# Third block of the seven-product FFN heads into the hand-written order, with earlier side sums and an earlier copy of x

## The chip, the cores and the metric

One Trainium2 chip, one of its cores. The metric is the device time of one execution of the whole program in microseconds (us). TensorE (PE in the profile) multiplies; VectorE (DVE), ScalarE (ACT) and GpSimd (POOL) work on what it needs and gives; the DMA queues of SyncE (SP) and of POOL move data. Each engine works through its own queue of instructions in order, and engines wait for one another by semaphores.

## The reference

A trunk of four layers on x, 512 positions by 1024 channels, float32. Each layer adds a mixer's output to x (layers 0 and 3: S5, layer 1: gated linear attention, layer 2: differential attention), and then a SwiGLU feed-forward (FFN) of hidden size 2816; a last rmsnorm ends it.

```python
def swiglu_ffn(h, w_gate_up, w_down):
    g, u = jnp.split(h @ w_gate_up, 2, axis=-1)
    return (jax.nn.silu(g) * u) @ w_down

for l in range(DEPTH):
    ...
    x = x + mixer(rmsnorm(x, ...))
    h = rmsnorm(x, ffn_norm_g[l])
    x = x + swiglu_ffn(h, ffn_w_gate_up[l], ffn_w_down[l])
```

The change concerns the FFNs of layers 1, 2 and 3: their first three of 11 blocks of 256 hidden channels.

## The kernel before

**Precision.** A float32 product is made of three products in the faster format fp32r: each operand is split into a high part (a copy with rounding, on ACT; for weights `high`, L334) and a low part (the operand minus its high part, on DVE; for weights `low`, L338), and high x high, high x low and low x high are summed. So every weight tile that TensorE uses costs one ACT and one DVE instruction of 128x1024 first, and the two matmul groups that need only the high part can start before the low part is there: each product's first two matmuls take the high part of the weights, the third the low part.

**Seven products.** Layer 0's FFN is `ffn_plain`. The FFNs of layers 1, 2 and 3 (`ffn`, L712) multiply 2x2 partitioned matrices with seven products instead of eight. `Sides` keeps the four quarters of the normed input, transposed (F), and makes the sums of them that the scheme needs (`total`, L191; high and low parts L212 and L217). `seven_block` (L571) holds the steps of one block: loads of weight quarters from DRAM (L599 by SP, or `staged`, L324), sums of quarters either by a DMA that accumulates (POOL's queue, L602) or on DVE (`add`, L659), splits, the products `one` to `seven` (each 24 matmuls of 128x256 on L566), and the evacuations: `one_out` (ACT copy, L638), `two_out` (DVE, L645), `gate1` and `gate2` (DVE multiply by the norm's scale L611, ACT SiLU L612), `five_out` and `six_out` (ACT copies, L656, L670), `seven_out` (DVE, L676), `three_out` (DVE subtraction L683 and multiply L684), and in `four_out` the multiply L693 and the split of the result into high and low (`act`, ACT copies L703 and DVE subtractions L704; in layer 2 in four pieces, since the columns change order there). PSUM banks: a for products one, six, seven, four; c for five and three; d for two.

**Order of the work.** In each of these FFNs the first two blocks, a and b, stand in an order written out by hand: `plan` in `ffn` is a list of step names, and all five queues (PE, ACT, DVE, SP, POOL) run in the order in which the steps issue instructions. `finish`, `square`, `diag`, `spread`, `rows`, `flush` and the `total`, `high`, `low` steps without a block letter belong to the norm and the sides. After `self.hand()` a planner orders the instructions of blocks 2 to 10 by due times. The blocks are done in groups of 4, 4 and 3; behind each group the down projection (`gemm_b`) runs. Weight tiles come from pools: `wst` (3 buffers, staged quarters), `whl` (5 buffers, split quarters), three `slots`, and rooms lent from `act` buffers, the quarters F once the sides are made, and the gain's buffer. A block's first quarter of weights can be loaded and split ahead of the FFN (`ahead`, L165), which also makes the first side sum, `total("3")`, when two blocks are done.

**x's copy.** Layer 2's FFN leaves its columns in another order for the S5 layer behind it. For that `turn_x` (L800) copies x to DRAM (L804, 2048 KB) and back with the rows in the other order (L806), and the norm's scale the same way (L808, L810), all four on POOL's queue; the way back waits for the way there. Before, this is issued behind the accumulating load of the third block's product three (`self.added`).

**Ahead of the head.** The attention's last product of layer 2 is ordered by hand as well: its four row tiles are evacuated by `evac` and the FFN's first weights made ready by `ahead(1)` between the products (`between`). Layers 1 and 3 call `ahead(2)` in the last product of their mixers (L1521, L1734).

Of the kernel before, what the change touches and what calls it, by code (L numbers as in the profile page):

```python
# [11 lines left out]
F32 = mybir.dt.float32  # L12
F32R = mybir.dt.float32r
# [132 lines left out]
class Sides(Left):  # L146
# [18 lines left out]
    def ahead(self, n):  # L165

        w = [self.tr.staged(self.quarter(0, 0, b), 4, 256) for b in range(len(self.heads), len(self.heads) + n)]
        self.heads += [self.tr.halves(y, 4, 256) for y in w]
        if len(self.heads) == 2:
            self.total("3")  # L170
# [92 lines left out]
class Trunk:  # L263
# [307 lines left out]
    def seven_block(self, fp, slots, left, wgu, b, turn):  # L571
# [20 lines left out]
        def load(name, q, half, plus=None, room=None):  # L592
# [8 lines left out]
            if plus:  # L601
                self.added = nc.gpsimd.dma_start(w[:], left.quarter(*plus, b), accum_op=ALU.add)  # L602
# [78 lines left out]

        def three_out():
            v.tensor_tensor(keep["r2"][:], bank["c"][:], keep["r2"][:], op=ALU.subtract)  # L683
            v.tensor_tensor(keep["r1"][:], keep["r1"][:], keep["r2"][:], op=ALU.mult)  # L684
# [4 lines left out]

        def four_out():  # L690
            g2 = T("g2")
            scaled(g2, bank["a"], 1)
            v.tensor_tensor(keep["r5"][:], g2[:], keep["r5"][:], op=ALU.mult)  # L693
            act = fp.tile([P, 2, 2, SEQ], F32R, tag="act", name="act", bufs=4)
            for th, k in enumerate(("r1", "r5")):
                src = keep[k][:].rearrange("p (j n) -> p j n", j=2)
                if turn:
                    dst = act[:].rearrange("p z j (b h m) -> p z j h m b", b=4, h=2)[:, :, :, th]
                    src = src.rearrange("p j (m b) -> p j m b", b=4)
                else:  # L700
                    dst = act[:].rearrange("p z j (h n) -> p z j h n", h=2)[:, :, :, th]
                for j in range(2) if turn else (slice(None),):
                    nc.scalar.copy(dst[:, 0, j], src[:, j])  # L703
                    v.tensor_tensor(dst[:, 1, j], src[:, j], dst[:, 0, j].bitcast(F32), op=ALU.subtract)  # L704
            return act
# [3 lines left out]
            add, six, six_out, seven, seven_out, three, three_out, four, four_out,  # L709
        )}  # L710

    def ffn(self, l, left, after=None, turn=False, aside=None):  # L712
# [5 lines left out]
        with self.tc.tile_pool(name=f"ffn{l}", bufs=1, reuse_waits="tile") as fp:  # L718
# [11 lines left out]
            f = blocks[:2]  # L730
            if l == 3:
                left.open(fp, ("4", "3", "22"))
            for w, n, *room in (
# [6 lines left out]
                split21a one:a split21b square flush one:b total1 one_out:a finish high1 low1 total2 split1a high2 low2  # L740
                one_out:b two:a two:b split1b high3 two_out:a five:a add22a highSa two_out:b lowSa five_out:a five:b
                add22b highSb diag lowSb low3 split3a six:a spread five_out:b rows six:b six_out:a split3b seven:a
                six_out:b total4 split22a high4 low4 seven:b seven_out:a split22b three:a seven_out:b gate1:a gate1:b
                high22 low22 three:b add21a highFa add21b lowFa highFb lowFb four:a four:b three_out:a three_out:b
            """
            for step in plan.split():
                name, _, n = step.partition(":")
                if n:
                    f["ab".index(n)][name]()
                elif name[-1] in "ab":  # L750
                    word = next(w for w in ("split", "add", "high", "low") if name.startswith(w))
                    w = name[len(word) : -1]
                    f["ab".index(name[-1])][word]({"S": "1", "F": "1"}.get(w, w))
# [4 lines left out]
                elif name == "flush":  # L758
                    self.flush()
                else:  # L760
# [4 lines left out]
            F = left.freed()  # L765
            slots[:] = [F[0], F[1], slots[0], F[2], left.g[:].rearrange("p (k n) -> p k n", n=256), F[3]] + slots[1:]
            b0 = 0
            for nb in (4, 4, 3):
                acts = []
                for n in range(b0, b0 + nb):  # L770
                    b = blocks[n]
                    if n > 1:
                        for w in ("direct", "room1", "room22", "room21", "summed"):
                            b[w]()
                    if turn and n == 2:

# [1013 lines left out]
    def diff(self, l, left, after):  # L1790
# [4 lines left out]
        with self.tc.tile_pool(name="diff", bufs=1) as p:  # L1795
# [268 lines left out]
            for t in range(2, NT):  # L2064
# [6 lines left out]
                if t == 2:  # L2071
                    nxt[0].ahead(1)
# [65 lines left out]
```

## Time and profile before

| what | us |
|---|---|
| median of 3 runs | 2381.13 (2380.29 to 2392.86) |
| the profiled execution | 2382.31 |
| span of its trace | 2380.6 |
| mean granted TensorE clock | 0.982 of full |
| PE busy | 2269.0 |
| DVE busy | 1487.1 |
| ACT busy | 1073.0 |
| POOL busy | 266.8 |

The span is what the hardware profiler saw from the first to the last instruction; the execution's time holds 1.7 us more around it. A row of a timeline reads: start, duration of the stretch, engine, line, operation, tile written <- tiles read, shapes, how many instructions; in brackets how long the engine had been idle before it and which instruction released it ("<-ACT whl L334" is the end of a high part of weights). A row of a group has count, busy time, mean ns of one, and idle time before with its releasers. A row of DMA issues has count, size and median us from issue to landing. In the trace the products are known by their bank and sides: "c<-side" is three, "d<-sides" two, "a<-sides" one or, with "side", six, seven or four, and "c<-side" in a block's second place five.

### The profile page before, as it was taken

The page shows a single profiled execution, that of the slowest core. Times are in us where ns is not written, and L with a number is a line of the kernel's source. Part 1 is how long each engine was busy: PE and PEld are TensorE (multiplying, and loading weights), DVE is VectorE, ACT ScalarE, POOL GpSimd, SP SyncE. Part 2 cuts the span into 40 slices and gives each one's busy share as a digit, 9 for nine tenths or more (in the row PEclk, how much of TensorE's full clock was granted, in tenths as well). Part 3 has the DMA queues.
Part 4 walks back from the last instruction along what each step waited for, and adds up shares of the span by engine and source line. Part 5 has one row for each costly group of instructions (what it writes and reads, how often), then busy time and mean ns, then how long its engine had stood idle before and what let it go on. Part 6 is the DMA issues. An engine that isn't in the chain of part 4 may idle for free. (4 is left out here: it accounts for less than half of the span.)

```text
span 2380.6 us, 35208 instructions
## 1 busy us (share of the span) xinstructions
PE 2269.0 (95%) x14055; PEld 1962.8 (82%) x14055; DVE 1487.1 (62%) x2311; ACT 1073.0 (45%) x1749; POOL 266.8 (11%) x335
## 2 busy tenths in 40 slices
PE   4799999999999999999999998989999899999997
PEld 3578888788877789898987887888989788999996
DVE  7774565555443459585753666875847874967674
ACT  4463445444352346252544665653635233634442
POOL 3330100111000011010001221110000000101000
PEclk9699999999999999999999999999999899999999
DMA  4123344544332258564345465694732645666521
GB/s 110 34 52 138 95 138 143 166 129 166 118 103 85 71 143 208 137 177 124 111 142 117 107 133 145 170 243 115 195 98 89 214 158 150 170 179 154 162 76 67
DMA packets 275502, 317.42 MB, mean 133 GB/s; under 512 B 45653, under 2 KB 214377, under 8 KB 274058
## 3 DMA queue, kind: packets, MB, share of 16 engines
q1 hardware_dynamic: 227210, 238.14, 31.9%
q0 software_dynamic: 48128, 77.02, 15.7%
q8 instruction: 111, 1.82, 0.3%
q14 instruction: 53, 0.43, 0.1%
HBM read 275.92 MB, written 23.99 MB: 126 GB/s over the span
## 5 line engine op out<-in xcount | busy, mean ns | idle before, releaser
L338 DVE TENSOR_TENSOR whl<-wst,whl 128x1024 fp32r<-128x1024 f32 x294 | 359.0, 1223 | 363.1 <-ACT whl L334 362.3
L334 ACT CAST whl<-wst 128x1024 fp32r<-128x1024 f32 x294 | 308.4, 1050 | 530.5 <-PE acc L353 354.8
L566 PE MATMUL a<-side,whl 128*128 128x256 f32 x2376 | 291.2, 279 | 14.2 <-ACT r L638 6.0
L566 PEld LDWEIGHTS a<-side,whl 128*128 128x128 f32 x2376 | 281.4, 190 | 16.2 <-ACT whl L334 6.9
L351 PE MATMUL acc<-whl,act 128*128 128x512 f32 x704 | 276.5, 393 | 0.7 <-DVE g L611 0.7
L353 PE MATMUL acc<-whl,act 128*128 128x512 f32 x704 | 276.9, 393 | 0.0
L352 PE MATMUL acc<-whl,act 128*128 128x512 f32 x704 | 275.6, 391 | 0.0
L566 PE MATMUL c<-side,whl 128*128 128x256 f32 x1584 | 192.4, 278 | 3.6 <-DVE whl L338 3.6
L566 PEld LDWEIGHTS c<-side,whl 128*128 128x128 f32 x1584 | 186.9, 189 | 4.0 <-DVE whl L338 4.0
L351 PEld LDWEIGHTS acc<-whl,act 128*128 128x128 f32 x704 | 132.2, 188 | 30.9 <-DVE g L611 1.9
L352 PEld LDWEIGHTS acc<-whl,act 128*128 128x128 f32 x704 | 132.2, 188 | 28.8
L353 PEld LDWEIGHTS acc<-whl,act 128*128 128x128 f32 x704 | 132.3, 188 | 27.9
L351 PE MATMUL any<-hT,whl 128*128 128x512 f32 x384 | 151.7, 395 | 0.0
L352 PE MATMUL any<-hT,whl 128*128 128x512 f32 x384 | 149.6, 390 | 0.0
L353 PE MATMUL any<-hT,whl 128*128 128x512 f32 x384 | 149.6, 389 | 0.0
L351 PE MATMUL acc<-whl,hT 128*128 128x512 f32 x352 | 143.8, 408 | 1.1 <-ACT whl L334 0.6
L352 PE MATMUL acc<-whl,hT 128*128 128x512 f32 x352 | 138.6, 394 | 1.0 <-DVE whl L338 1.0
L353 PE MATMUL acc<-whl,hT 128*128 128x512 f32 x352 | 139.0, 395 | 0.0
L338 DVE TENSOR_TENSOR whl<-halves,whl 128x1024 fp32r<-128x1024 f32 x72 | 87.7, 1222 | 32.5 <-ACT whl L334 32.5
L352 PE MATMUL acc<-whl,zT 128*128 128x512 f32 x256 | 103.9, 406 | 4.1 <-DVE whl L338 4.1
L334 ACT CAST whl<-halves 128x1024 fp32r<-128x1024 f32 x72 | 75.3, 1052 | 69.2 <-PE acc L353 26.7
L351 PE MATMUL acc<-whl,zT 128*128 128x512 f32 x256 | 102.8, 406 | 2.7 <-ACT zT L468 2.7
(438 smaller groups left out, 4185.1 us busy)
## 6 DMA issues: line engine op xcount, KB each, us to landing
wst<-in_ffn_w_gate_up_dram SPq DMA_DIRECT2D x110, 512.0 KB, 4.0
wst<-in_ffn_w_down_dram SPq DMA_DIRECT2D x88, 512.0 KB, 3.7
halves<-in_ffn_w_gate_up_dram SPq DMA_DIRECT2D x42, 512.0 KB, 5.9
slot<-in_ffn_w_gate_up_dram SPq DMA_DIRECT2D x39, 512.0 KB, 6.6
wst<-in_ffn_w_gate_up_dram POOLq DMA_DIRECT2D x33, 512.0 KB, 6.4
wst<-in_s_w_glu_dram SPq DMA_DIRECT2D x32, 512.0 KB, 3.6
spill<-opsp POOLq DMA_DIRECT2D x8, 2048.0 KB, 8.7
wst<-in_gla_w_in_dram SPq DMA_DIRECT2D x24, 512.0 KB, 3.6
```

Source lines behind the costliest of these rows:

```text
L334: self.nc.scalar.copy(hl[:, 0], w[:])
L338: self.nc.vector.tensor_tensor(hl[:, 1], w[:], hl[:, 0].bitcast(F32), op=ALU.subtract)
L351: mm(out, lh, rh, start=first, stop=False)
L352: mm(out, lh, rl, start=False, stop=False)
L353: mm(out, ll, rh, start=False, stop=last)
L566: mm(o, hl[:, x, k, c], side[:, y, k], start=first and not (j or k or n), stop=k == 3 and n == 2, skip_group_check=True,)
```

## The change

- The plan goes on through the third block, c: its loads, its splits, its products (in the order one, five, two, six, seven, three, four), its side sums and most of its evacuations are written out. Two of c's quarters are loaded into F(0,0) and F(0,1) (steps F0 and F1), which come free inside the plan.
- `three_out` and `four_out` are split into steps. The evacuations of a and b (gate1, three_sub, three_mul, gate2, half1, four_mul, half2) stand behind c's first weight splits, instead of ahead of four:a or right behind four:b.
- Side 22's high and low (high22, low22) and the sums for four (add21a, add21b) stand ahead of the gate1 steps.
- total3 is no longer part of `ahead`: in layers 1 and 3 it is called behind `ahead(2)`, in layer 2 it stands in the plan behind one:b.
- x's copy stands in the plan behind five:b.
- In the attention's last product the evacuations of the first two tiles stand two matmul groups sooner, and `ahead(1)` stands behind the evacuations of the third and fourth tile.

The number of instructions on each engine is the same in both kernels. In the order on TensorE only block c differs: before, the planner had placed it as one, five, two, six, with two and six interleaved, then seven, three, four; after the change four:c's first two matmuls are followed by the first two of block d's one.

```diff
--- before.py
+++ after.py
@@ -166,8 +166,6 @@
 
         w = [self.tr.staged(self.quarter(0, 0, b), 4, 256) for b in range(len(self.heads), len(self.heads) + n)]
         self.heads += [self.tr.halves(y, 4, 256) for y in w]
-        if len(self.heads) == 2:
-            self.total("3")
 
     def open(self, pool, names):
 
@@ -599,7 +597,7 @@
                 nc.sync.dma_start(W[name][:], left.quarter(q, half, b))
             w = W[name]
             if plus:
-                self.added = nc.gpsimd.dma_start(w[:], left.quarter(*plus, b), accum_op=ALU.add)
+                nc.gpsimd.dma_start(w[:], left.quarter(*plus, b), accum_op=ALU.add)
 
         def done(name):
             if name not in lent:
@@ -679,34 +677,60 @@
             product("4", "22", bank["c"], False)
             done("22")
 
+        def three_sub():
+            v.tensor_tensor(keep["r2"][:], bank["c"][:], keep["r2"][:], op=ALU.subtract)
+
+        def three_mul():
+            v.tensor_tensor(keep["r1"][:], keep["r1"][:], keep["r2"][:], op=ALU.mult)
+
         def three_out():
-            v.tensor_tensor(keep["r2"][:], bank["c"][:], keep["r2"][:], op=ALU.subtract)
-            v.tensor_tensor(keep["r1"][:], keep["r1"][:], keep["r2"][:], op=ALU.mult)
+            three_sub()
+            three_mul()
 
         def four():
             product("22", "1", bank["a"], False)
             done("1")
 
+        def gate2():
+            keep["g2"] = T("g2")
+            scaled(keep["g2"], bank["a"], 1)
+
+        def four_mul():
+            v.tensor_tensor(keep["r5"][:], keep["g2"][:], keep["r5"][:], op=ALU.mult)
+
+        def half(th, k):
...
+            for j in range(2) if turn else (slice(None),):
+                nc.scalar.copy(dst[:, 0, j], src[:, j])
+                v.tensor_tensor(dst[:, 1, j], src[:, j], dst[:, 0, j].bitcast(F32), op=ALU.subtract)
+
+        def half1():
+            half(0, "r1")
+
+        def half2():
+            half(1, "r5")
+            return keep["act"]
+
+        def act():
+            return keep["act"]
+
         def four_out():
...
+            gate2()
+            four_mul()
+            half1()
+            return half2()
 
...
@@ -727,7 +751,8 @@
                 lent = room()
             self.jobs = aside(fp) if aside else iter(())
             blocks = [self.seven_block(fp, slots, left, wgu, b, turn) for b in range(FFN_HIDDEN // 256)]
-            f = blocks[:2]
+            f = blocks[:3]
+            F = left.freed()
             if l == 3:
                 left.open(fp, ("4", "3", "22"))
             for w, n, *room in (
@@ -737,46 +762,50 @@
                 f[n][w](*room)
 
             plan = """
-                split21a one:a split21b square flush one:b total1 one_out:a finish high1 low1 total2 split1a high2 low2
-                one_out:b two:a two:b split1b high3 two_out:a five:a add22a highSa two_out:b lowSa five_out:a five:b
-                add22b highSb diag lowSb low3 split3a six:a spread five_out:b rows six:b six_out:a split3b seven:a
-                six_out:b total4 split22a high4 low4 seven:b seven_out:a split22b three:a seven_out:b gate1:a gate1:b
-                high22 low22 three:b add21a highFa add21b lowFa highFb lowFb four:a four:b three_out:a three_out:b
+                split21a one:a split21b square flush one:b total3 total1 one_out:a finish high1 low1 total2 F0 room1:c
+                split1a high2 low2 one_out:b two:a two:b split1b high3 two_out:a five:a add22a highSa two_out:b lowSa
+                five_out:a five:b turn add22b highSb diag lowSb low3 split3a six:a spread five_out:b rows six:b six_out:a
+                split3b seven:a direct:c six_out:b total4 F1 split22a high4 low4 seven:b seven_out:a split22b high22 low22
+                room22:c three:a room21:c high11c add21a highFa add21b lowFa highFb three:b lowFb summed:c seven_out:b
+                four:a low11c high1c gate1:a three_sub:a four:b three_sub:b low1c one:c
+                three_mul:a gate2:a half1:a four_mul:a half2:a split21c one_out:c five:c add22c gate1:b highSc three_mul:b
+                lowSc two:c five_out:c six:c split3c gate2:b half1:b four_mul:b half2:b two_out:c gate1:c
+                six_out:c seven:c split22c seven_out:c three:c add21c highFc three_sub:c lowFc three_mul:c four:c
             """
+            if l != 2:
+                plan = plan.replace("total3", "")
             for step in plan.split():
                 name, _, n = step.partition(":")
                 if n:
-                    f["ab".index(n)][name]()
-                elif name[-1] in "ab":
+                    f["abc".index(n)][name]()
+                elif name in ("F0", "F1"):
+                    slots.append(F[int(name[1])])
+                elif name[-1] in "abc":
                     word = next(w for w in ("split", "add", "high", "low") if name.startswith(w))
                     w = name[len(word) : -1]
-                    f["ab".index(name[-1])][word]({"S": "1", "F": "1"}.get(w, w))
+                    f["abc".index(name[-1])][word]({"S": "1", "F": "1"}.get(w, w))
                 elif name in ("finish", "diag", "spread", "rows"):
                     getattr(left, name)()
                 elif name == "square":
                     left.square(NT - 1, 1)
                 elif name == "flush":
                     self.flush()
+                elif name == "turn":
+                    r = self.turn_x(left.r) if turn else r
                 else:
                     word = next(w for w in ("total", "high", "low") if name.startswith(w))
                     getattr(left, word)(name[len(word) :])
             self.hand()
 
-            F = left.freed()
-            slots[:] = [F[0], F[1], slots[0], F[2], left.g[:].rearrange("p (k n) -> p k n", n=256), F[3]] + slots[1:]
+            slots[:] = [F[2], *slots[:2], left.g[:].rearrange("p (k n) -> p k n", n=256), F[3]] + slots[2:]
             b0 = 0
             for nb in (4, 4, 3):
                 acts = []
                 for n in range(b0, b0 + nb):
                     b = blocks[n]
-                    if n > 1:
+                    if n > 2:
                         for w in ("direct", "room1", "room22", "room21", "summed"):
                             b[w]()
-                    if turn and n == 2:
-
-                        with self.tc.issue_after(self.added.ins):
-                            r = self.turn_x(left.r)
-                    if n > 1:
                         for step in ("one", "one_out", "five", "five_out"):
                             b[step]()
                         b["add"]("22")
@@ -784,7 +813,7 @@
                             b[step]()
                         b["add"]("21")
                         b["four"]()
-                    acts.append(b["four_out"]())
+                    acts.append(b["four_out"]() if n > 1 else b["act"]())
                     next(self.jobs, None)
                 stat = lambda k, part, t: acts[k // 2][:, part, k % 2, t * P : (t + 1) * P]
                 if nb == 3 and after is not None:
@@ -1518,7 +1547,7 @@
                         evac_b(t, accs[t])
                 else:
                     self.gemm_b(stat, wg, KT, D + d * 512, evac_b)
-                ahead = (lambda: nxt.ahead(2)) if L and d else None
+                ahead = (lambda: (nxt.ahead(2), nxt.total("3"))) if L and d else None
                 self.gemm_b(stat, wg, KT, d * 512, evac_a, tail=4 if d else 0, ahead=ahead)
         return nxt
 
@@ -1731,7 +1760,7 @@
             for d in range(2):
                 self.gemm_b(
                     so, wo, KT, d * 512, self.add_x(d, nxt), tail=4 if d else 0, between=() if d else late,
-                    ahead=(lambda: nxt.ahead(2)) if d else None,
+                    ahead=(lambda: (nxt.ahead(2), nxt.total("3"))) if d else None,
                 )
         return nxt
 
@@ -2058,8 +2087,8 @@
                 unit(t, KT - 1)
             one = lambda: self.pend.pop(0)()
             between = {
-                2: {1: (one,), 3: (one, lambda: evac(0, banks[0])), 5: (one, lambda: evac(1, banks[1])), 7: (one,)},
-                3: {1: (one,), 3: (one, lambda: nxt[0].ahead(1)), 5: (one,)},
+                2: {1: (one, lambda: evac(0, banks[0])), 3: (lambda: evac(1, banks[1]), one), 5: (one,), 7: (one,)},
+                3: {1: (one,), 3: (one,), 5: (one,)},
             }
             for t in range(2, NT):
                 banks.append(self.acc())
@@ -2068,8 +2097,7 @@
                     for f in between[t].get(k, ()):
                         f()
                 evac(t, banks[t])
-                if t == 2:
-                    nxt[0].ahead(1)
+                nxt[0].ahead(1)
             self.lazy = False
         return nxt[0]
 
```

26 lines of the change are left out of this document (10 added, 16 removed).

## The prediction

> **What bounds the kernel now.** I read the page's first part, then windows of the trace (columns: window, its length, busy us and instructions of PE, weight loads, DVE, ACT, POOL, then granted clock, DMA share, GB/s), then TensorE's timeline around the hand-ordered heads of the three seven-product FFNs, then groups and DMA issues.
>
> ```profile
> span 2380.6 us, 35208 instructions
> ...
> PE 2269.0 (95%) x14055; PEld 1962.8 (82%) x14055; DVE 1487.1 (62%) x2311; ACT 1073.0 (45%) x1749; POOL 266.8 (11%) x335
> ```
>
> ```profile
> 912.00:944.00 32.00, 28.49 (x237) 27.66 (x237) 31.27 (x37) 21.06 (x26) 5.16 (x4) 1.00 0.96 240
> 1050.00:1080.00 30.00, 30.00 (x263) 30.00 (x262) 23.80 (x27) 17.05 (x21) 2.56 (x2) 1.00 0.73 196
> 1515.00:1530.00 15.00, 15.00 (x132) 14.93 (x131) 13.75 (x18) 10.12 (x15) 1.33 (x1) 1.00 0.37 77
> 1555.00:1560.00 5.00, 5.00 (x31) 4.92 (x31) 3.86 (x4) 2.05 (x3) 1.12 (x2) 0.69 0.96 259
> 1560.00:1565.00 5.00, 5.00 (x44) 5.00 (x44) 4.66 (x5) 5.00 (x7) 1.31 (x1) 1.00 1.04 433
> ```
>
> TensorE is the bound: 95% of the span. In the steady FFN (1050 to 1080) it never stops: 30.00/263 = 0.114 us a matmul, so 24 x 0.114 = 2.74 us a product. In the head of layer 1 (912 to 944) it has 28.49 of 32, and VectorE 31.27: there VectorE sets the pace. TensorE's timeline shows the holes. Heads of layers 1, 2 and 3:
>
> ```profile
> 905.87 5.60 PE L566 MATMUL c<-side,whl 128*128 128x256 f32 x48
> 913.43 0.50 PE L566 MATMUL a<-side,whl 128*128 128x256 f32 x2 [1.95 <-ACT whl L334]
> 914.69 5.49 PE L566 MATMUL a<-side,whl 128*128 128x256 f32 x46 [0.76 <-DVE whl L338]
> ...
> 955.54 2.88 PE L566 MATMUL c<-side,whl 128*128 128x256 f32 x24
> ```
>
> ```profile
> 1534.30 5.60 PE L566 MATMUL c<-side,whl 128*128 128x256 f32 x48
> ...
> 1554.51 4.39 PE L566 MATMUL c<-side,whl 128*128 128x256 f32 x22 [2.79 <-DVE whl L338]
> ...
> 1584.54 5.02 PE L566 MATMUL a<-side,whl 128*128 128x256 f32 x24 [6.04 <-ACT r L638]
> ...
> 1595.00 2.88 PE L566 MATMUL c<-side,whl 128*128 128x256 f32 x24
> ```
>
> ```profile
> 2054.84 5.60 PE L566 MATMUL c<-side,whl 128*128 128x256 f32 x48
> 2062.40 0.50 PE L566 MATMUL a<-side,whl 128*128 128x256 f32 x2 [1.96 <-ACT whl L334]
> 2063.66 6.94 PE L566 MATMUL a<-side,whl 128*128 128x256 f32 x46 [0.76 <-DVE whl L338]
> ...
> 2104.82 2.88 PE L566 MATMUL c<-side,whl 128*128 128x256 f32 x24
> ```
>
> In each fence the first row holds three:a and three:b, the last is three:d. From three:b (first row + 2.74) to three:d lie 15 products, without a hole 41.04 us. Measured: 955.54 - 908.61 = 46.93, 1595.00 - 1537.04 = 57.96, 2104.82 - 2057.58 = 47.24. So the heads lose **5.9, 16.9 and 6.2 us**, 29 in all: more than that the reordering can't gain. About 3 us of each is the wait ahead of four:a: in layer 1 its last 46 matmuls start at 914.69 instead of 911.35 + 2 x 0.114, in layer 3 the waits are the same (1.96 + 0.76).
>
> Durations, and what two instructions of a queue take start to start:
>
> ```profile
> 905.23 1.22 DVE L338 TENSOR_TENSOR whl<-gain,whl 128x1024 fp32r<-128x1024 f32 x1
> 906.96 1.28 DVE L611 TENSOR_TENSOR r<-r,R 128x512 f32<-128x512 f32 x2
> 911.02 2.35 DVE L659 TENSOR_TENSOR lent<-lent,slot 128x1024 f32<-128x1024 f32 x2
> ```
>
> ```profile
> L338 DVE TENSOR_TENSOR whl<-halves,whl 128x1024 fp32r<-128x1024 f32 x7 | 8.4, 1219 | 0.5 <-ACT whl L334 0.5
> L334 ACT CAST whl<-halves 128x1024 fp32r<-128x1024 f32 x7 | 7.3, 1051 | 3.8 <-PE c L566 2.3 <-DVE halves L659 0.7 <-ACT whl L334 0.7
> L703 ACT CAST act<-r 128x512 fp32r<-128x512 f32 x5 | 3.1, 619 | 3.3 <-DVE r L684 1.7 <-DVE r L693 1.6
> L611 DVE TENSOR_TENSOR g<-a,R 128x512 f32<-128x512 f32 x3 | 2.0, 683 | 0.0
> L612 ACT ACTIVATE g<-g 128x512 f32<-128x512 f32 x3 | 1.9, 632 | 1.3 <-DVE g L611 1.2
> ```
>
> VectorE back to back: 2.35 - 1.22 = 1.13 (I take 1.14) a wide one, 1.28 - 0.68 = 0.60 a 512 one; an isolated one ends 1.22 or 0.68 after its start. ACT: high part 1.05, copy 0.62, SiLU 0.63. I charge 0.05 us to hand over between engines.
>
> **Part 1, sides and four:a.** The number of instructions stays. low22 goes ahead of seven_out:b and the gate1s, so VectorE starts it at 905.23 + 1.14 = 906.36, the two sums at 907.50 and 908.64; ACT's highFa runs 908.77 to 909.82, lowFa starts 909.87. four:a, wanted at 908.61 + 2.74 = 911.35, waits no longer: **3.0 us gone** per head. What moves back behind it is what is late next.
>
> **Part 2, the third block behind the evacuations.** From lowFb's end to lowFc VectorE now has 9 wide (9 x 1.14 = 10.3) and 19 narrow (19 x 0.60 = 11.4) instructions: 21.7 us, against 8 products x 2.74 = 21.9. So throughput is just enough, and each wait of VectorE for ACT shows on TensorE. The new order is full of them: a multiply, ACT's SiLU, ACT's copy, a subtraction, a multiply, ACT's copy, a subtraction, and only then the next weights. Laying each queue's instructions of layer 1 one behind another with the durations above:
> - gate2:a ends 918.11, SiLU to 918.79, copy to 919.36, subtraction 919.41, four_mul to 920.69, copy to 921.36; ACT's high21c 921.27 to 922.32, low21c to 923.59. two:c was wanted at 922.37; its first two matmuls run, the rest starts 923.64: **1.1 lost**.
> - gate1:b ends 925.33, SiLU 926.01, highSc 927.01, lowSc 928.28; six:c's rest at 928.33 instead of 926.3: **2.0 lost**.
> - gate2:b ends 930.32, SiLU, copy (to 931.57), four_mul ends 932.90, copy 933.57, two_out, gate1:c ends 935.50, SiLU 936.18, six_out, high22c 936.61 to 937.66, low22c to 938.93; three:c's rest at 938.98 instead of 933.8: **5.2 lost**.
> - add21c follows low22c to 940.67, highFc 941.77, lowFc 943.52: four:c **1.6 lost**.
>
> Sum 9.9, and block d has no hole: three:d at 908.61 + 41.04 + 9.9 = 959.5. Layer 1 loses 9.9 - 5.9 = **+4.0**. Layer 3 has the same instructions and shapes: 9.9 - 6.2 = **+3.7**.
>
> **Part 3, layer 2 and x's copy.** Here the act halves are copied in four pieces:
>
> ```profile
> 1548.39 2.27 ACT L703 CAST act<-r 128x256 fp32r<-128x256 f32 x4
> ```
>
> The copies start (2.27 - 0.58)/3 = 0.56 apart, so a pair of halves costs about 1 us more: two:c loses 2.1, six:c 2.0, three:c 6.0, four:c 1.4, and 0.9 is left in d: 12.4. The wait of 6.04 ahead of six:d (row 1584.54) goes, if its cause goes:
>
> ```profile
> 1580.64 1.04 ACT L334 CAST whl<-wst 128x1024 fp32r<-128x1024 f32 x1 [7.09 <-DMA wst<-in_ffn_w_gate_up_dram]
> 1533.68 1.30 POOL L804 DMA_DIRECT2D xturn<-vall  x1
> 1555.97 0.57 POOL L806 DMA_DIRECT2D x<-xturn  x1 [12.53 <-DMA xturn<-vall]
> xturn<-vall POOLq DMA_DIRECT2D x1, 2048.0 KB, 22.0
> x<-xturn POOLq DMA_DIRECT2D x1, 2048.0 KB, 10.5
> xkeep<-x POOLq DMA_DIRECT2D x1, 2048.0 KB, 11.5
> spill<-opsp POOLq DMA_DIRECT2D x8, 2048.0 KB, 8.7
> ```
>
> ACT holds a cast of ready-made order behind 7.09 us of DMA, and its one_out behind that holds TensorE. The copy lay in the busiest stretch (share 0.96 to 1.04). Now it is issued behind five:b, about 1519.5, where the share was 0.37. Its price there isn't in the trace; the nearest rows of 2048 KB are 8.7 and 11.5 below, 22.0 above. I take 10 for the first, as spill and xkeep, and 10.5 for the second: landed about 1540, and the third block's sum 3:c, queued behind it on POOL, lands about 1550, against high3c at about 1557. So the copy hides, and d's loads have the queue free. Layer 2: 12.4 - 16.9 = **-4.5**. At its start, total3 leaves VectorE's queue ahead of total1, but the side casts that follow are paced by VectorE all the same (13.75 of 15, window 1515): 0, between -1.7 and +1. The earlier evacuations in the attention's last product cost 0, hidden behind TensorE, with those same ends.
>
> The Trainium skill (DMA: Bandwidth & Descriptors, Anatomy of one DMA) fits software-queued DMAs by 2.0 us plus bytes over 436e3: for 2 MB 6.8 us, an estimate. The rows here, 8.7 to 22.0, all lie above; by the page the copy would be done by about 1534 and nothing else in the sum would move.
>
> **Part 4, the clock.** After the 2.79 us wait at 1554.5 the granted clock was 0.69 for 5 us, with 31 matmuls instead of 45: 14 x 0.114 = 1.6 us. The holes of 1.95 and 0.76 cost nothing of it in layer 1 (46 matmuls in 5.49) and 1.4 in layer 3 (46 in 6.94). The new hole at three:c, 5.2 to 6.0 us, is longer than both in each head: 3 x 1.6 = **+4.8** (ends: 0, and 3 x 2.1 by row 1584.54, where 24 matmuls took 5.02 instead of 2.88 after 6 us).
>
> The Trainium skill (TensorE: Matmul & The Clock Gate, section HAM oscillation) asks for no TensorE gap over about 3.4 us. The trace is stricter, since 2.79 sufficed at 1554.5; the page speaks against this change as well, since three:c's hole is over its figure in all three heads: with it as without it 4.8 us.
>
> **Sum.** +4.0 - 4.5 + 3.7 + 4.8 = **+8.0**. The profiled execution took 2382.31 (span 2380.6); with it 2390.3. It lay 1.2 above the median shown, 2381.13, so I forecast **2389**.
>
> **Rivals.**
> - *The hand-overs cost nothing.* If two queues overlap better than laid end to end, all holes of part 2 go: -5.9 - 16.9 - 6.2 = -29, of which layer 2's four-piece copies and d's rest keep some 5 to 8: -22, **2359**. For it: throughput is enough (21.7 against 21.9), and VectorE was busy 31.27 of 32 before, so the old order had hardly a wait for ACT. Against it: each new wait is a true dependence, and L612's group shows ACT idle 1.2 us waiting for its multiply even now. Chance 0.10.
> - *VectorE's total work sets the heads either way.* It was busy 31.27 of 32; the same instructions in another order take as long, holes included: layers 1 and 3 stay, without new clock drops, layer 2 gains the 6.0 wait and the 2.1 behind it: -8, **2373**. Against it: the new order makes VectorE wait. Chance 0.13.
> - *Slower: POOL's queue stands behind x's copy.* The return copy waits for the first to land, and all POOL issues behind it (the sums 3:c and for d) wait too. If the price is that of the rows, 22.0 and 10.5, the last of turn's four DMAs issues at 1519.5 + 22 + 10.5 = 1552, and 3:c's sum, 10 to 12 us later, is about 7 us late for high3c: 2389 + 7 = **2396**. It decides from an issue later than about 1547. For it: the only row of this transfer says 22. Against it: that was at a share of 0.96. Chance 0.17.
>
> **How the numbers follow.** Forecast 0.60, rivals 0.10, 0.13, 0.17. Half a per cent, 12 us, is about what a measurement of this kernel can tell from no change: 2369.2 and 2393.0. The forecast's own range, 2380 to 2397, has the clock's ends (-4.8 and +1.5), some 4 either way for the unpriced starts of layer 2 and the hole estimates, and upward 2.4 more if a hand-over is 0.10 instead of 0.05 us (16 in a head's chain, three heads); a quarter of its chance lies above 2393, none below 2369. The faster case is below, the VectorE case between, two thirds of the slower one above: faster 0.10, same 0.45 + 0.13 + 0.06 = 0.64, slower 0.26. The range goes from 2371 (below the VectorE case) to 2399 and leaves out the faster case and the slower one's upper end, under 0.2.
>
> **What would show it.** In the changed kernel's heads: four:a without a wait for whl; waits for whl from DVE ahead of two:c, six:c, three:c (about 5 us, the longest) and four:c; VectorE idle behind ACT, under 80% busy in 912 to 944; a clock under 1 after three:c; three:d at about 961 (with the clock), 1592, 2110. In layer 2: xturn issued about 1519 and landed in 12 us or less, no 6 us wait before six:d, 3:c's sum landed by 1556. It is wrong if VectorE stays over 95% busy with no waits at three:c (then faster), or if high3c waits for a DMA (then the third rival).

## The result, and the profile after

The changed kernel takes 2402.1 us (median of 8 runs, 2397.48 to 2410.63) against 2382.81 for the kernel before in the same comparison: a ratio of **1.0079** (95% interval 1.0062 to 1.0095), or 18.8 us more (14.8 to 22.6). The forecast was 8 us more, 2389, in a range that ended at 2399. The sign was right, the size was not.

The profiled execution took 2408.28, at the upper end of its eight, so it is read for places and not for the total; a second trace of the same kernel (run r1 below, its execution 2402.28) is set beside it where the size counts. TensorE's timeline of layer 1's head, three:a to three:d, as for the kernel before:

```profile
910.14 5.60 PE L564 MATMUL c<-side,whl 128*128 128x256 f32 x48
915.58 5.60 PE L564 MATMUL a<-side,whl 128*128 128x256 f32 x48
921.02 3.02 PE L564 MATMUL a<-sides,whl 128*128 128x256 f32 x24
923.88 2.90 PE L564 MATMUL c<-side,whl 128*128 128x256 f32 x24
926.78 0.51 PE L564 MATMUL d<-sides,whl 128*128 128x256 f32 x2
928.04 2.90 PE L564 MATMUL d<-sides,whl 128*128 128x256 f32 x22 [0.76 <-DVE whl L336]
931.38 0.50 PE L564 MATMUL a<-side,whl 128*128 128x256 f32 x2 [0.44 <-ACT whl L332]
932.64 2.79 PE L564 MATMUL a<-side,whl 128*128 128x256 f32 x22 [0.76 <-DVE whl L336]
941.07 5.07 PE L564 MATMUL a<-side,whl 128*128 128x256 f32 x24 [5.64 <-ACT r L668]
945.98 2.89 PE L564 MATMUL c<-side,whl 128*128 128x256 f32 x24
...
967.07 2.88 PE L564 MATMUL c<-side,whl 128*128 128x256 f32 x24
```

four:a (915.58) follows three:b without a wait, as intended. Then two:c, six:c and above all seven:c (941.07) wait, and seven:c runs at half clock: 5.07 us instead of 2.9, with a granted clock of 0.55 over 941 to 946. From three:b (910.14 + 2.74) to three:d lie 54.2 us, 41.04 of them work: 13.2 lost, where the kernel before lost 5.9. The same rows of layers 2 and 3:

```profile
1547.32 5.60 PE L564 MATMUL c<-side,whl 128*128 128x256 f32 x48
...
1582.28 5.30 PE L564 MATMUL a<-side,whl 128*128 128x256 f32 x24 [8.78 <-ACT r L668]
...
1609.10 2.88 PE L564 MATMUL c<-side,whl 128*128 128x256 f32 x24
```

```profile
2069.00 5.60 PE L564 MATMUL c<-side,whl 128*128 128x256 f32 x48
...
2099.91 5.49 PE L564 MATMUL a<-side,whl 128*128 128x256 f32 x24 [5.64 <-ACT r L668]
...
2126.70 2.88 PE L564 MATMUL c<-side,whl 128*128 128x256 f32 x24
```

They lose 18.0 (before 16.9) and 13.9 (before 6.2). What seven:c waits for is L668, six_out:c, ACT's copy of bank a. Here is ACT's and VectorE's part of the timeline ahead of it:

```profile
933.93 0.68 DVE L609 TENSOR_TENSOR g<-a,R 128x512 f32<-128x512 f32 x1
...
934.71 0.64 ACT L610 ACTIVATE g<-g 128x512 f32<-128x512 f32 x1 [1.95 <-DVE g L609]
935.25 0.60 ACT L712 CAST act<-r 128x512 fp32r<-128x512 f32 x1
935.88 0.69 DVE L713 TENSOR_TENSOR act<-r,act 128x512 fp32r<-128x512 f32 x1 [1.27 <-ACT act L712]
936.49 0.69 DVE L699 TENSOR_TENSOR r<-g,r 128x512 f32<-128x512 f32 x1
937.21 0.62 ACT L712 CAST act<-r 128x512 fp32r<-128x512 f32 x1 [1.36 <-DVE r L699]
937.86 0.69 DVE L713 TENSOR_TENSOR act<-r,act 128x512 fp32r<-128x512 f32 x1 [0.69 <-ACT act L712]
938.47 0.68 DVE L643 TENSOR_TENSOR r<-r,d 128x512 f32<-128x512 f32 x1
939.18 0.69 DVE L609 TENSOR_TENSOR r<-r,R 128x512 f32<-128x512 f32 x1
939.91 0.63 ACT L610 ACTIVATE r<-r 128x512 f32<-128x512 f32 x1 [2.08 <-DVE r L609]
940.45 0.57 ACT L668 COPY r<-a 128x512 f32<-128x512 f32 x1
940.91 1.05 ACT L332 CAST whl<-halves 128x1024 fp32r<-128x1024 f32 x1
```

Each engine's brackets name the other: gate2:b, its SiLU, copy, subtraction, multiply, copy, subtraction, two_out, gate1:c, its SiLU, and only then six_out and, last, the cast of side quarter 22's weights for three:c (940.91), though its bank was ready at about 935.4 (six:c's end: 932.64 + 2.79).

```profile
929.00:949.00 20.00, 13.03 (x89) 12.22 (x87) 10.89 (x15) 7.78 (x12) 1.28 (x1) 0.83 0.52 113
941.00:946.00 5.00, 4.93 (x25) 4.93 (x26) 1.23 (x1) 0.96 (x2) 0.00 (x0) 0.55 0.32 100
```

No engine is full there: of the 20 us from 929 to 949 TensorE has 13.03, VectorE 10.89, ACT 7.78. Two queues in strict order wait for each other in turn.

One more wait is new, behind the head: the first down projection stops inside.

```profile
973.29 1.06 ACT L332 CAST whl<-wst 128x1024 fp32r<-128x1024 f32 x1 [3.92 <-DMA wst<-in_ffn_w_down_dram]
...
974.25 0.61 ACT L712 CAST act<-r 128x512 fp32r<-128x512 f32 x1
...
975.52 0.69 DVE L713 TENSOR_TENSOR act<-r,act 128x512 fp32r<-128x512 f32 x1
976.12 0.69 DVE L609 TENSOR_TENSOR g<-a,R 128x512 f32<-128x512 f32 x1
...
976.86 0.50 PE L349 MATMUL acc<-whl,act 128*128 128x512 f32 x1 [2.13 <-DVE g L609]
```

ACT's cast waits for a load of down weights; block d's act copy stands behind it, then d's gate2 multiply, which frees bank a, and the projection needs that bank: 2.13 us. The same row before, 0.54:

```profile
963.74 0.50 PE L351 MATMUL acc<-whl,act 128*128 128x512 f32 x1 [0.54 <-DVE g L611]
```

To compare runs, this table gives for each FFN what TensorE lost from its first product to the first matmul of the down projection (that stretch minus 672 x 0.114 us for 28 products), then what it lost in the first projection (first to 192nd matmul, minus 191 x 0.2285). Half clock is in it. Each row is from one trace; the ratios are of all executions.

| kernel | heads of layers 1, 2, 3 | projections | sum | against before | ratio of times |
|---|---|---|---|---|---|
| before | 7.8, 20.8, 8.1 | 0.9, 0.3, 0.1 | 38.0 | | |
| changed | 15.0, 21.4, 15.8 | 2.5, 2.5, 3.8 | 61.0 | +23.0 | 1.0079 |
| changed, second trace (r1) | 15.1, 20.9, 15.1 | 2.0, 1.7, 1.1 | 55.9 | +17.9 | 1.0078 |
| e1 six_out:c sooner | 14.0, 19.4, 14.8 | 2.3, 5.1, 1.8 | 57.4 | +19.4 | 1.0063 |
| e2 weights first | 6.3, 15.7, 6.3 | 4.8, 4.6, 5.4 | 43.1 | +5.1 | 1.0002 |
| e3 copy early alone | 7.9, 13.7, 7.8 | 0.1, 0.3, 1.2 | 31.0 | -7.0 | 0.9961 |
| e5 sides sooner alone | 6.6, 17.4, 6.6 | 1.1, 1.3, 1.5 | 34.5 | -3.5 | 0.9978 |
| e6 changed, copy late | 14.5, 18.5, 14.5 | 2.3, 4.2, 2.6 | 56.6 | +18.6 | 1.0069 |
| e9 e3 and e5 together | 6.6, 11.9, 6.2 | 1.1, 0.9, 0.2 | 26.9 | -11.1 | 0.9948 |

The sum follows the measured times within some 5 us (the changed kernel +23.0 and +17.9 against +18.8, e9 -11.1 against -12.4): these stretches hold the effect.

The median of the kernel before lies between 2382.81 and 2387.30 in the comparisons below, so differences are worked out from the ratios, and the times that were expected before a run hold only to these few us.

### The profile page after: what moved, and what is told of

The parts are those of the page before. It is cut to its first block, busy times and chain, and to the rows that moved or that the text cites. A ratio compares the mean times of both kernels' runs of the same rounds, so it can differ in the third digit from the quotient of the medians.

```text
span 2406.6 us, 35212 instructions
## 1 busy us (share of the span) xinstructions
PE 2276.9 (95%) x14055; PEld 1967.7 (82%) x14055; DVE 1487.7 (62%) x2311; ACT 1072.1 (45%) x1749; POOL 267.1 (11%) x335
## 3 DMA queue, kind: packets, MB, share of 16 engines
q1 hardware_dynamic: 227210, 238.14, 31.9%
```

## The experiments

**Is it the bank, or the chain?** The theory is that the chain of hand-overs shown above sets the hole; the rival, that six_out's bank alone does. e1 moves one step ahead of the chain:

```diff
-            if b == 1:
+            if b in (1, 2):
                 keep["r2"] = self.np_.tile(...)
...
-  split3c gate2:b half1:b four_mul:b half2:b two_out:c gate1:c six_out:c seven:c
+  split3c gate2:b six_out:c half1:b four_mul:b half2:b two_out:c gate1:c seven:c
```

> The changed kernel with one step moved: six_out of block c stands right behind gate2:b instead of behind all evacuations of b (its result goes to a buffer of another pool, so that it needn't wait for one). Theory A (a chain of hand-overs between VectorE and ACT ahead of c's weights): the 5.6 us wait of seven:c goes below 1.5 us, but three:c then waits about 4.5 us for its weights, which stand behind the same evacuations; sum of the holes per head 10.3 instead of 11.0 us, the clock still drops: 2398 to 2404, the changed kernel's time within 3 us. Rival B (only the bank that six_out holds): no new hole at three:c, 8 us less per head (5.8 and 2.2 of half clock): about 2378.

Measured 2403.0 (1.0063, 1.0039 to 1.0086). TensorE's timeline of its layer 1:

```profile
929.75 3.00 PE L564 MATMUL a<-side,whl 128*128 128x256 f32 x24 [0.68 <-ACT r L668]
935.89 0.50 PE L564 MATMUL c<-side,whl 128*128 128x256 f32 x2 [3.14 <-ACT whl L332]
937.15 4.31 PE L564 MATMUL c<-side,whl 128*128 128x256 f32 x22 [0.76 <-DVE whl L336]
```

seven:c's wait falls to 0.68, and three:c, next in line, waits 3.14 and 0.76 for weights whose split stands behind the same chain. The hole has moved, as theory A had it, and the time has not by more than these intervals tell. The bank decides where TensorE stops, the chain how long.

**Weights ahead of evacuations.** e2 puts c's splits ahead of the evacuations that nothing needs yet. It also runs six:c ahead of two:c, has e1's buffer for six_out, and leaves the last evacuations of b and c to the planner.

```diff
-  four:b three_sub:b low1c one:c three_mul:a gate2:a half1:a four_mul:a half2:a split21c one_out:c five:c
-  add22c gate1:b highSc three_mul:b lowSc two:c five_out:c six:c split3c gate2:b half1:b four_mul:b ...
+  four:b three_sub:b low1c one:c five:c add22c highSc three_mul:a gate2:a lowSc half1:a one_out:c six:c
+  split21c two:c four_mul:a split3c five_out:c half2:a six_out:c gate2:b high22c seven:c low22c three:c ...
```

> The changed kernel with the same steps in another order: c's weight splits stand ahead of the evacuations of a and b wherever the evacuation isn't needed yet (six:c ahead of two:c, split3c and high22c ahead of b's act halves), and the last evacuations of b and c are left to the planner. Theory A: laid end to end with the row's durations, block c has no hole in layer 1 and 0.9 us in layer 2, so seven:c, three:c and four:c wait less than 1 us each and the clock doesn't drop; what is put off comes back in block d with 0 to 4 us a head: 2360 to 2374. Rival C (VectorE's work of the head is the bound in any order): the holes come back in d, 6 us or more a head: 2380 or more.

Measured 2387.87 (1.0002, 0.9989 to 1.0015): some 18 us faster than the changed kernel and equal to the kernel before. In layer 1 block c has no hole up to three:c, seven:c follows two:c at once (four:c waits 0.57 us):

```profile
925.10 3.02 PE L564 MATMUL d<-sides,whl 128*128 128x256 f32 x24
927.97 2.90 PE L564 MATMUL a<-side,whl 128*128 128x256 f32 x24
930.71 2.88 PE L564 MATMUL c<-side,whl 128*128 128x256 f32 x24
...
938.86 2.89 PE L564 MATMUL a<-sides,whl 128*128 128x256 f32 x22 [0.90 <-DVE whl L336]
...
964.90 0.79 PE L349 MATMUL acc<-whl,act 128*128 128x512 f32 x1 [3.15 <-DVE g L609]
```

But what was put off returns: 0.90 at one:d and others, 3.15 in the projection. Theory A's time, 2360 to 2374, was missed. The time was the one that rival C named, though not by C's way alone: layer 1's head itself lost 6.3 instead of 7.8, and the projections lost 14.8 instead of 1.3 in all.

**The two parts that could be had alone.** e3 is the kernel before with x's copy behind five:b, e5 the kernel before with side 22 and the sums for four ahead of the gate1 steps, e9 both.

```diff
-  five_out:a five:b add22b
+  five_out:a five:b turn add22b
...
-  split22b three:a seven_out:b gate1:a gate1:b high22 low22 three:b add21a highFa add21b lowFa highFb lowFb four:a
+  split22b high22 low22 three:a add21a highFa add21b lowFa highFb three:b lowFb seven_out:b gate1:a gate1:b four:a
```

> The kernel before with x's copy alone moved behind five:b. Theory D (the copy delayed the loads of block d): the 6.0 us wait ahead of block d's six goes and the 2.1 us of half clock behind it: 2373 to 2377. Rival E (the copy's place only decides which loads are late): as much is lost at the third block's weights, which then load beside the way back of x: 2380 to 2385.

> The kernel before with side 22 and the sums for four alone moved ahead of the gate1 steps (block c stays with the planner, the evacuations of a and b stand right behind seven_out:b and four:b). Theory A (order and hand-overs count): the 2.7 to 3.1 us ahead of four:a go in each of three heads and under 1 us of them comes back: 2373 to 2376. Rival C (VectorE's work is the bound, 31.27 of 32 us busy): what four:a gains is lost again at c's first products, at most its idle 0.7 to 2 us a head are won: 2377 to 2382.

> The kernel before with the two parts that gained alone: side 22 and the sums for four sooner, and x's copy behind five:b; block c stays with the planner. If the parts are independent: 9.5 and 5.4 us less than before, 2366 to 2371. Rival (VectorE's work bounds layer 2's head, so that only the larger one counts there): 2371 to 2375.

e3: 2377.07 (0.9961, 0.9946 to 0.9976), 9.3 us less, as theory D had it; the 6.0 us wait ahead of block d's six is gone, and the copy took 9.0 us there, not 22.0:

```profile
xturn<-vall POOLq DMA_DIRECT2D x1, 2048.0 KB, 9.0
```

e5: 2381.04 (0.9978, 0.9965 to 0.9991), 5.2 us less. four:a's wait of about 3 us is gone, but five:c's grew from 0.84 to 2.38 and its 22 matmuls took 4.39 us instead of 2.77. By the table 1.2 and 1.5 us are left in the heads of layers 1 and 3, so more than half came back: between the theory and rival C.

```profile
916.08 5.60 PE L566 MATMUL a<-side,whl 128*128 128x256 f32 x48
...
927.16 4.39 PE L566 MATMUL c<-side,whl 128*128 128x256 f32 x22 [2.38 <-DVE whl L338]
```

e9: 2372.22 (0.9948, 0.9934 to 0.9963), 12.4 us less than before, the fastest kernel here and some 31 us faster than the changed one. The parts add up to most of their sum (14.5); in layer 2 five:c now waits 4.31. Beside it stands e2, which holds the same two parts, writes block c out and has the rest of the change: some 13 us slower, and its projections lose 14.8 us where e9's lose 2.2. So even with the weights first, the third block written out costs more here than the planner's order of it.

**x's copy inside the changed kernel.** e6 puts the step turn back behind summed:c.

```diff
-  five_out:a five:b turn add22b
+  five_out:a five:b add22b
...
-  three:b lowFb summed:c seven_out:b
+  three:b lowFb summed:c turn seven_out:b
```

> The changed kernel with x's copy put back behind the third block's last accumulating load, as in the kernel before. Theory D (the early copy is good here too): the third block's sum lands in time, so seven:c's wait falls from 8.8 to about 6.9 us, but the loads of block d stand beside the copy again and lose 4 to 8 us: 2404 to 2409. Rival F (in the changed kernel it is the early copy that delays the third block): the 2 us are won and nothing is lost: 2398 to 2400.

Measured 2402.61 (1.0069, 1.0053 to 1.0086), no difference that these intervals tell. seven:c's wait in layer 2 fell from 8.78 to 6.48, the copy's two transfers took 15.3 and 15.9 us, and block d had no 6 us wait either way; the projection there lost 4.2 instead of 2.5. So in the changed kernel the early copy does cost the third block some 2 us, as rival F said, but to put it back gained nothing that the times show: neither F's 2398 to 2400 nor D's loss in block d came.

**The projection's wait.** Two edits aimed at the loads of down weights: e12 issues those of the first group on POOL's queue, e14 and e15 (the changed kernel and e2) hold the fifth block's loads behind the fourth of them.

```diff
-        self.nc.sync.dma_start(w[:], src)
+        (self.nc.gpsimd if self.down else self.nc.sync).dma_start(w[:], src)
```

```diff
+  with self.tc.issue_after(down[0].ins) if n == 4 else ExitStack():
       for w in ("direct", "room1", "room22", "room21", "summed"):
           b[w]()
```

> The changed kernel with the down projection's weights of the first group of blocks loaded by POOL's queue instead of SP's. Theory G (those loads stand in SP's queue behind a slot load that waits for its slot, ACT's cast waits for them ahead of block d's act copy, and so bank a of d comes free late): the wait inside the first down projection, 2.1 us a head, falls under 0.8, 4 to 6 us less than the changed kernel: 2396 to 2399. Rival H (VectorE's put-off work or the bank itself): the wait stays, 2400 to 2404.

> The changed kernel with the loads of the fifth block (the first of the next group) held behind the fourth down projection load of the first group, so that no slot load that waits for its slot stands ahead of these four on a queue. Theory G (the down projection's wait of 2.1 us a head comes from loads that stand behind such a slot load): the wait falls under 0.8 in each head, 4 to 6 us less than the changed kernel: 2396 to 2399. Rival H (VectorE's put-off work keeps bank a of block d): the wait stays at 1.8 to 2.3 us, 2400 to 2404.

> The order with c's weights first (the second experiment), with the fifth block's loads held as in the run beside this one. There the down projection loses 4.6 to 5.4 us a head. Theory G: these go to under 1.5 us each, 10 to 13 us less: 2374 to 2379. Rival H: VectorE is behind by the put-off evacuations, the wait stays over 3 us: 2384 to 2390.

e12 took 2420.11 (1.0140, 1.0123 to 1.0157), the wrong way: the loads came later still, ACT's cast waited 5.04 us, and the projection 5.21.

```profile
976.81 1.05 ACT L334 CAST whl<-wst 128x1024 fp32r<-128x1024 f32 x1 [5.04 <-DMA wst<-in_ffn_w_down_dram]
```

```profile
980.37 0.80 PE L351 MATMUL acc<-whl,act 128*128 128x512 f32 x1 [5.21 <-DVE g L611]
```

A later load goes with a longer wait of the projection. Theory G's reason, a slot load in the queue ahead, isn't borne out: e14 took 2405.83 (1.0085, 1.0065 to 1.0105), with waits of 1.25, 3.00 and 2.48 us in the three layers, and e15 2390.04 (1.0010, 0.9994 to 1.0027), with 2.02, 2.78 and 3.42, and there was no gain in the sum (60.9 and 42.3 by the table's count). The traces show another reason. The load for which the cast at 973.29 waited went out as soon as a low part on VectorE had freed its buffer (`wst` has three), though SP's issue before it had ended at 963.88:

```profile
964.53 1.22 DVE L336 TENSOR_TENSOR whl<-wst,whl 128x1024 fp32r<-128x1024 f32 x1
965.79 2.10 SPq L322 DMA_DIRECT2D wst<-in_ffn_w_down_dram  x2
```

In the kernel before, the load in the same place went out at 953.01:

```profile
953.01 12.88 SPq L324 DMA_DIRECT2D wst<-in_ffn_w_down_dram  x5
```

It is so in every head of the kernel before, the changed one, e2, e14 and e15. Counted back from the projection's first matmul, this load went out 7.7 to 8.0 us ahead in the kernel before and in e9 (waits of 0 to 0.71), 6.4 to 6.7 in the changed kernel (1.81 to 2.13) and 6.0 to 6.1 in e2 (2.64 to 3.50). That points to the work put off on VectorE, as rival H said; no run takes that work away, so this is read from the traces and not shown by an experiment.

**The clock.** A filler of matmuls whose result nothing reads, 48 ahead of seven:c (72 in layer 2), was run twice, the second time beside the changed kernel.

```diff
-  six_out:c seven:c
+  six_out:c warm seven:c
...
+  elif name == "warm":
+      idle = self.tp("idle")
+      y = left.place["3"][:, 0]
+      for k in range(72 if turn else 48):
+          self.nc.tensor.matmul(idle[:, 0:2], y[:, k % 4, :P], ...)
```

> The changed kernel with matmuls that compute nothing used (48 ahead of seven:c, 72 in layer 2), written to a bank that nothing reads, so that TensorE isn't idle there. Theory I (the hole of 5.6 us itself halves the clock afterwards): the wait stays as filler, seven:c's 24 matmuls take 2.7 instead of 4.8 us, 2.2 us a head less: 2394 to 2397. Rival J (seven:c is slow for another reason): 2400 to 2404, with the added matmuls maybe more.

> The changed kernel once more, beside the next run on the same chip, to price the clock. As before: 16 to 21 us over the kernel before, seven:c's matmuls at half clock for about 2.2 us in each head.

> The changed kernel with the filler matmuls ahead of seven:c once more, on the same chip as the run beside it. In the trace of the first such run the heads lost 6.3 us less, and the time didn't fall. Theory I (the saved half clock is worth what the heads show): 4 to 7 us less than the changed kernel beside it. Rival K (clock that is saved in the heads is lost elsewhere, in other drops or in the projection's waits): within 2 us of it.

```profile
940.67 4.98 PE L564 MATMUL a<-side,whl 128*128 128x256 f32 x24 [5.64 <-ACT r L668]
```

```profile
935.12 5.92 PE L797 MATMUL idle<-side 128*128 128x256 f32 x48
940.92 3.01 PE L564 MATMUL a<-side,whl 128*128 128x256 f32 x24
```

The first row is the changed kernel's (r1), the others have the filler (second run): seven:c takes 3.01 us, not 4.98, so the idle hole is what halves the clock, and it costs 1.2 to 2.1 us a head (heads 13.0, 19.7, 13.1 against 15.1, 20.9, 15.1 beside it). Yet the times were 2404.86 (1.0081, 1.0064 to 1.0099) in the first run, and 2402.5 (1.0075, 1.006 to 1.009) against 2403.86 (1.0078, 1.0063 to 1.0094) in the second: 5.4 us fewer in the heads, 1.4 fewer in the time. The intervals are some 3.6 us wide either way, so whether the saving is lost elsewhere or lies within the noise isn't settled. In these two traces 4.3 us of it go in a stretch that the filler doesn't touch, from the first projection of layer 1 to layer 2's head (495.9 and 500.2 us), but that stretch took 496 to 502 us over all fourteen traces.

## Why the prediction missed

The direction, the place and most of the mechanism were right; the size was not. In the traces the heads to three:d lost +7.3, +1.1 and +7.7 (13.2, 18.0 and 13.9 against 5.9, 16.9 and 6.2), and the projections' waits +1.6, +2.1 and +1.8: together +21.6, where the sum had 8.0. The second trace has +7.3, +0.6 and +7.0 in the heads and, by the table's count, +3.5 in the projections: +18.4, close to the measured +18.8. So 7 to 8 us were missed in the heads and 3.5 to 5.5 behind them. Two steps failed:

- **The sum ended at three:d.** Block d had no hole of any size, as forecast, but the sum had no term for what follows it: the down projection waited 2.13, 2.11 and 1.81 us, 5.5 more than before (3.5 in the second trace). I had followed the loads of x's copy, not those of the down weights. A late head alone is not the reason: e2's head of layer 1 loses less than the kernel before's, and its projections lose 14.8 us in all. Why these loads go out late is read above from the traces alone.
- **Slower matmuls were mis-sized.** Taken from start to start, a matmul that starts late with TensorE idle before it is a wait; what else is over 0.114 us a matmul is a slower matmul, in the changed kernel mostly at a lower clock. The new waits came to 31.9 us in the three heads (33.5 in the second trace), against 9.9 + 12.4 + 9.9 = 32.2 in the sum. But the 29 us that the sum took off were 20.5 of waits and 8.6 of slower matmuls, and it put only 4.8 of the second sort back (part 4); they came to 13.2 (10.4).

Part by part:

- **Part 1** held. four:a waits in no head, and e5 shows that alone the earlier sides are worth 5 us in the three heads.
- **Part 2**, laying the queues end to end, was good to a few tenths. With the 4.27 us by which this trace was late already (three:a at 910.14 instead of 905.87; layer 1's first product starts anywhere from 874 to 881 in the fourteen traces), two:c's rest was forecast at 927.91 and came at 928.04, six:c's at 932.60 and came at 932.64, high22c at 940.88 and came at 940.91. Its third bullet failed in one point: it let seven:c run during the hole and stopped three:c. But seven adds into bank a, which six_out:c must copy first, so TensorE stopped one product sooner, for 5.64 us. By e1 that alone costs almost nothing.
- **Part 3** was wrong by 4 us (3.5 in the second trace). The -4.5 had layer 2's three:c hole at 6.0; seven:c waited 8.78. That layer 2's waits still came to 12.7 in the first trace, against 12.4, is luck: six:c's forecast 2.0 was missing there, because two:c ran at half clock (22 matmuls in 4.39 us). x's copy went as forecast (issued at 1533.2, or 1520.2 without the 13.0 by which this trace's three:a was late there; 10.0 and 9.3 us), but the rest of the third rival's mechanism came in part:

```profile
1558.16 0.56 POOL L839 DMA_DIRECT2D rturned<-rturn  x1 [13.12 <-DMA rturn<-rcol]
1561.98 1.33 POOL L600 DMA_DIRECT2D wst<-in_ffn_w_gate_up_dram  x1 [3.27 <-DVE act L713]
```

```profile
1545.40 5.01 SPq L322 DMA_DIRECT2D wst<-in_ffn_w_gate_up_dram  x2
```

```profile
1572.09 1.06 ACT L332 CAST whl<-wst 128x1024 fp32r<-128x1024 f32 x1 [2.20 <-DMA wst<-in_ffn_w_gate_up_dram]
```

  The way there of the small scale vector (2 KB) lay in POOL's queue behind x's way back and took 13.6 us to land, and POOL stood 13.12 us for it. It was free at 1558.72, but the third block's sum went out only at 1561.98, 0.7 us behind the landing of the load that it adds to. SP had issued that load right beside x's way back, at 1545.40, and it was 15.9 us under way; in e6, with the copy later, its like took 6.6 us. (The row names VectorE's L713, which ended about then; but in the kernel before and in e6 the sum went out 1.0 us behind the same landing, so I take it to be that.) The sum landed just ahead of the cast at 1572.09: 1559.1 on the old scale, where 1550 was forecast and 1557 needed. So SP's loads were slow beside the copy too, which the third rival didn't have. e6 confirms the 2 us. And e3 shows that the copy's place is worth 9 us in the kernel before, which is why the -4.5 looked safe; in the changed kernel it is worth nothing that e6 shows. The earlier evacuations in the attention's last product and the later total3 cost nothing, as forecast: layer 2's stretch from its first product to three:a took 30.8 us (31.3 before), and the one ahead of it, from the first projection of layer 1, 497.9 and 495.9 (497.5 before). No run has these two alone.
- **Part 4**: each hole does halve the clock, for 1.8 to 2.6 us (seven:c's start to three:c's, less 2.74, in both traces) and not 1.6. Short waits can do it as well, or not: after 0.90 and 0.76 us ahead of two:c in layer 2 its 22 matmuls took 4.39 us in the first trace and 2.90 in the second. The Trainium skill (TensorE: Matmul & The Clock Gate, section HAM oscillation) warns of gaps over about 3.4 us; the 5.64 and 8.78 us here agree. That the 4.8 is paid in the total isn't shown.
- **The rivals**: that hand-overs cost nothing is refuted by the waits in the rows, by e1, where the wait goes with the chain, and by e2, where another order takes 18 us off. That VectorE's work sets the pace in any order is half true: in the changed kernel the order made it wait (23.64 us busy in 912 to 944, where it had 31.27), e2, with the same work in a better order, ends where the kernel before does, and e5 and e9 show that more is to be had.

In the range, the error was to widen by what bounded the terms that I had, and by nothing for the stage behind them.

## What to carry to other kernels

When steps of a strict order are put off, write down for each product not only its weights but the bank it writes and who must read that bank first, and follow the sum to the first instruction of the next stage, its loads included. An evacuation that hops between two engines costs its full chain where it stands ahead of a weight split that is needed soon. To put the splits first took 18 us off here, but what is put off comes due at the next stage, and e2 ended no better than the kernel before. Of a change in several parts, the cheap ones (here an earlier side sum and an earlier copy, 12 us less together) may be worth more without the large one.

## What the runs showed of the hardware

- A TensorE gap of 5.6 us was followed by a product at half clock (5.07 us instead of 2.9, granted clock 0.55 over 5 us); matmuls of no use in the gap kept the clock (3.01 us), but the time fell by 1.4 us at most where 5.4 were saved in these stretches.
- The same 2048 KB copy on POOL's queue took 22.0 us in the kernel before, where it ran beside the loads of the blocks behind, 9.0 to 10.0 behind five:b, and 15.3 behind the third block's loads. A 2 KB copy queued behind its way back took 13.6 us to land, and a 512 KB load on SP's queue, issued beside that way back, 15.9.
